# Update sums in the rows' own tiles, Fourier weights split ahead, and kept rows moved into the Fourier output projection

## The chip, the cores and the metric

The kernel runs on one core of a Trainium2 chip. The metric is the device time of one execution in microseconds (us); of several runs the median is given. The profile is one execution recorded by the hardware profiler. Engine names as the profile has them: PE is TensorE, PEld its weight loads, DVE is VectorE, ACT is ScalarE, POOL is GpSimd, SP is SyncE, which here only issues DMAs.

## The reference

Two layers on 512 latent tokens of 1024 channels (and 256 context tokens in layer 0). Each layer is: half-step SwiGLU FFN (width 2816), a token mixer, another half-step FFN. The mixer of layer 0 is windowed attention, that of layer 1 a Fourier mix. Each sub-layer's input is modulated, its output gated, added to the scaled input and normalised:

```
def post_norm_update(x, y, mod, j, g, b):
    gate = mod[:, 3 * j + 2][:, None, :]
    return layer_norm(ALPHA * x + gate * y, g, b)

def fourier_mix(h, w_o):                       # layer 1
    hg = h.reshape(B_, L_, FOURIER_GROUPS, FOURIER_GROUP_CH)     # 4 groups of 256 channels
    f = jnp.fft.fft2(hg, axes=(1, 3), norm="ortho").real
    return f.reshape(B_, L_, D_) @ w_o
...
        x = half_ffn_sublayer(x, mod_lat, 0, ffn_wi[i, 0], ffn_wo[i, 0], g[0], b[0])
        h = modulate(x, mod_lat, 1)
        y = ...                                # attention or fourier_mix
        x = post_norm_update(x, y, mod_lat, 1, g[1], b[1])
        x = half_ffn_sublayer(x, mod_lat, 2, ffn_wi[i, 1], ffn_wo[i, 1], g[2], b[2])
```

## The kernel before

All products are in float32 accuracy from three products of rounded halves: an operand is split into a high half (ScalarE copy, tiles `wh`, `uh`, `hh`, `ah`) and a low half (VectorE subtraction, `wl`, `ul`, `hl`, `al`), and `mm3` does high x high, low x high and high x low. Tokens are worked in four tiles of 128 rows. Helpers record every instruction, so the profile gives one line (L68) for nearly all; one goes by tile names.

**Slots.** Nearly all tiles in SBUF come from one pool of 42 equal slots (`SLOTS`, tag `slot`). A tile's slot comes free when its last reader is done; whoever needs one next waits for that. The pool also serves the raw weight loads, so loads are issued as slots come free.

**Weights.** `plan` lists all weight rows in the order of use: for the second layer the FFN's rows, then `w_t1` (one DFT table along channels), `w_t2` (four DFT tables along tokens), `w_fo` (eight rows of the Fourier output weights), then the last FFN. `weights(i, ahead)` (L176) makes sure that item i + ahead has been split, and loads raw rows (`wr`) two further. `gate_next` (L168) multiplies a raw row by a gate row (`wr<-wr,gr`) where a gate is folded into the weights, as it is for `w_fo`.

**Projection.** `project` (L459) computes y = u w: for the first rows f (the body) each row's product for all four token tiles, and the last `TAIL` = 4 rows token tile by token tile. Behind each token tile come `norm_stage` (L305: the sum `z` = ALPHA x + y and its statistics), `scale_stage` (z normalised in place) and `flip_stage` (products `tp` that turn it, the affine step `ht`, halves `hh` and `hl` for the next sub-layer). `z` is a slot of its own. In the body the look-ahead grows:

```
            self.weights(w0 + f, ahead=max(SPLIT_AHEAD, min(tail + 4, SPLIT_AHEAD + f - (body - 6))))
```

`project` returns two functions. `flip` turns the last token tile and is called during the next stage's first products. `keeps` loads two rows (`ln_g_row`, `ln_b_row`) and calls `keep_stage` (L372), which writes the new residual x = z g + b, two VectorE operations per token tile. In FFNs that follow, `keeps` is called at fixed pairs.

**Fourier stage** (L1135). Products `ab` with the channel table, evicted to `ah`, `al` and the Nyquist column `nyq`; then for each of four groups the cosine and sine products `f` along the tokens (group 0 also `pn` for the Nyquist rows), combined by four VectorE operations into `X`, with an edge row from `edge`. `stat` splits X of the group before into `uh` and `ul`. In this stage VectorE and ScalarE are pinned to the order of the code (`nc.pin(True)`); outside it a planner may move their instructions to where it expects a gap, within the dependencies. TensorE and GpSimd are pinned throughout. In that order stand, ahead of the groups, the split of the fourth token table and of `w_fo` rows 0 to 2 (`self.weights(w_fo + 2, ahead=0)`, L1177), and behind group 0 all four tiles of kept rows (`rest[1]()`, L1221). Then `project(w_fo, ...)` follows with a body of four rows.

Of the kernel before, what the change touches and what calls it, by code (L numbers as in the profile page):

```python
# [10 lines left out]
F32 = mybir.dt.float32  # L11
# [4 lines left out]
P = 128  # L16
D = 1024
KC = D // P
BLK = 32
BANK = 512  # L20
SEQ = 512
NT = SEQ // P
# [3 lines left out]
NF = DFF // P  # L26
# [13 lines left out]
SPLIT_AHEAD = 3  # L40
# [12 lines left out]
BETWEEN = 5  # L53
Q_TURN = 3
KEEP_AT = (5, 7, 9, 11)


class Pinned:
# [42 lines left out]
class Emitter:  # L101
# [203 lines left out]
    def norm_stage(self, st, t):  # L305
        nc = self.nc
        y, x = st["y"][t], st["x"][t]
        z = self.slot([P, 1024], F32, "z")
        stats = self.small([P, 2, 6], "bs")
        for h in range(2):  # L310
            sl = slice(h * 512, (h + 1) * 512)
            if "gate" in st:
                nc.vector.tensor_tensor(z[:, sl], y[:, sl], st["gate"][:, sl], ALU.mult)
                nc.vector.scalar_tensor_tensor(z[:, sl], x[:, sl], ALPHA, z[:, sl], ALU.mult, ALU.add)
            else:
                nc.vector.scalar_tensor_tensor(z[:, sl], x[:, sl], ALPHA, y[:, sl], ALU.mult, ALU.add)
            nc.vector.bn_stats(stats[:, h, :], z[:, sl])
        mv = self.small([P, 2], "mv")
        nc.vector.bn_aggr(mv, stats.rearrange("p a b -> p (a b)"))
        ve = self.small([P, 1], "ve")  # L320
        nc.vector.tensor_scalar(ve, mv[:, 1:2], EPS, None, ALU.add)
        rs = self.small([P, 1], "rs")
        nc.gpsimd.tensor_tensor(rs, ve, self.mhalf[:, 0:1], ALU.pow)
        st["n"][t] = (z, mv, rs)
# [131 lines left out]
                self.mod_steps(goal - self.n_job)  # L456


    def project(self, w0, nf, stat, st, ntok, mid=None, keep=True):  # L459
        mm = self.mm  # L460
        st["y"] = {}
        st["n"] = {}
        ss = {}

        def one(f, t, halfs=(0, 1)):
            w_hi, w_lo = self.parts[w0 + f]
            s_hi, s_lo = ss[f]
            if t not in st["y"]:
                st["y"][t] = self.bank2(nm="y")
            y = st["y"][t]  # L470
            sl = slice(t * P, (t + 1) * P)
            for i, (s, w) in enumerate(((s_hi, w_hi), (s_hi, w_lo), (s_lo, w_hi))):
                for half in halfs:
                    cs = slice(half * 512, (half + 1) * 512)
                    mm(y[:, cs], s[:, sl], w[:, cs], start=(f == 0 and i == 0), stop=(f == nf - 1 and i == 2))

        tail = TAIL if st["affine"] is not None else LAST_TAIL
        body = nf - tail
        for f in range(body):
            self.weights(w0 + f, ahead=max(SPLIT_AHEAD, min(tail + 4, SPLIT_AHEAD + f - (body - 6))))  # L480
            ss[f] = stat(f)
            if f == body // 2 and mid is not None:
                mid()
            for t in range(ntok):
                one(f, t)
            self.parts.pop(w0 + f)
        for f in range(body, nf):
            self.weights(w0 + f, ahead=nf + 3 - f)
            ss[f] = stat(f)
        self.nc.pin(st["affine"] is not None)  # L490
        for t in range(ntok):
            for half in range(2):
                for f in range(body, nf):
                    one(f, t, (half,))
            self.norm_stage(st, t)
            if st["affine"] is None:
                self.out_stage(st, t)
            elif t == 0:
                self.scale_stage(st, t)
            else:  # L500
                self.flip_stage(st, t - 1, lambda: self.scale_stage(st, t))
        self.nc.pin(False)
        for f in range(body, nf):
            self.parts.pop(w0 + f)

        def flip():
            v, a = self.nc.vector.on, self.nc.scalar.on
            self.nc.pin(True)
            self.flip_stage(st, ntok - 1)
            self.nc.vector.on, self.nc.scalar.on = v, a  # L510

        def keeps(i=None):

            if keep:
                if not i:
                    st["rows"] = self.ln_rows(*st["ln"])
                for t in range(ntok) if i is None else (i,):
                    self.keep_stage(st, t)

        return flip, keeps  # L520
# [21 lines left out]
        lo = self.hbuf([P, KC, SEQ], nm + "l")  # L542
        return [(hi, lo, 0, KC)]

    def half_step(self, ups, down, h, x, N, l, s, j, nxt, quota, first=None, halves=False, held=None, mid=None, out_h=None, keep=True, fold=True, more=None):

        us = []
        stat = self.halves_of(us, N)
        st = {}

        def late():
            self.mod_finish(self.n_job)
            gate = self.gate_row(l, s, j, 0.5)
            if fold:
                self.fold(gate, down, NF)
            else:
                st["gate"] = gate
            if more is not None:
                self.fold(self.gate_row(*more[0], 1.0), more[1], KC)
            stat(0)  # L560

        self.ffn_up(ups, h, N, quota, us, first=first, halves=halves, late=late, held=held)
        st["x"] = x() if callable(x) else x

        st["ln"] = (l, j)

        def middle():
            if mid is not None:
                mid()
            if keep and nxt is None:  # L570
                st["rows"] = self.ln_rows(l, j)

        st["affine"] = None if nxt is None else self.affine_ln(l, j, nxt[0], s, nxt[1])
        if nxt is not None:
            st["h"] = out_h() if out_h is not None else self.new_h("h")
        rest = self.project(down, NF, stat, st, N // P, mid=middle, keep=keep)
        return rest, st


# [135 lines left out]
    def run(self):  # L715
# [31 lines left out]
        w_l2 = ffn_items(2)  # L747
        w_t1 = add(ins["dft1"])
        w_t2 = add(*[ins["dft2"][i] for i in range(4)])
        w_fo = add(*[ins["fourier_wo"][k] for k in range(KC)])  # L750
# [9 lines left out]
        h, held = self.head()  # L760
# [7 lines left out]
        x = []  # L768
# [10 lines left out]
        def ctx_input():  # L779
# [17 lines left out]
        rest, st = self.half_step(  # L797
            w_l0[0], w_l0[1], h, load_x, SEQ, 0, 0, 0, (0, 1), 5 * KC, held=held, mid=ctx_input
        )
# [10 lines left out]
        def ctx_h():  # L810
# [11 lines left out]
        st = dict(x=x)  # L822
# [4 lines left out]
        rest = self.project(w_ao, KC, self.halves_of(oT, SEQ, KC), st, NT)  # L827
# [3 lines left out]
            w_l1[0], w_l1[1], st["h"], x, SEQ, 0, 0, 2, (1, 0), 5 * KC, first=rest, halves=True  # L831
        )
        rest, st = self.half_step(
            w_l2[0], w_l2[1], st["h"], x, SEQ, 1, 0, 0, (1, 1), 5 * KC, first=rest, halves=True, more=((1, 0, 1), w_fo)
        )

        fT = self.fourier(w_t1, w_t2, w_fo, st["h"], rest)
        st = dict(x=x)
        st["affine"] = self.affine_ln(1, 1, 1, 0, 2)
        st["h"] = self.new_h("h")  # L840

        st["ln"] = (1, 1)
        rest = self.project(w_fo, KC, fT, st, NT)


        rest, st = self.half_step(
# [288 lines left out]
    def fourier(self, w_t1, w_t2, w_fo, h, rest):  # L1135
# [38 lines left out]
        ny = (self.slot([P, NT, P], F32R, "nyh"), self.slot([P, NT, P], F32R, "nyl"))  # L1174
        self.split(ny[0], ny[1], nyq)
        t2 = [self.weights(w_t2 + i, ahead=3 - i) for i in range(4)]
        self.weights(w_fo + 2, ahead=0)  # L1177
        zero = self.slot([1, 256], F32, "zero")
        nc.gpsimd.memset(zero, 0.0)
        nh = SEQ // 2  # L1180
# [11 lines left out]
        for gr in range(FG):  # L1192
            ps, sine = (self.bank("f") for _ in range(2))
            for part, o in enumerate((ps, sine)):
                cs = slice(part * half, (part + 1) * half)

                def ops(t):
                    ah, al = ab[gr // 2, t // 2]
                    return ah[:, t % 2, gr % 2, cs], al[:, t % 2, gr % 2, cs]

                along(o[:, :n2], part, ops)
            if gr == 0:
                pn = self.bank("pn")
                along(pn[:, :n2], 0, lambda t: (ny[0][:, t], ny[1][:, t]))
            X = XX[:, gr]
            nc.scalar.copy(X[:, :, nh : nh + 1], ps[:, nh : nh + 1].unsqueeze(1).broadcast_to([P, 2, 1]))
            qs = self.slot([P, nh], F32, "qs")
            nc.scalar.copy(qs, sine[:, :nh])
            for i, (near, far) in enumerate(((ALU.subtract, ALU.add), (ALU.add, ALU.subtract))):
                nc.vector.tensor_tensor(X[:, i, :nh], ps[:, :nh], qs, near)  # L1210
                nc.vector.tensor_tensor(X[:, i, nh + 1 :], ps[:, nh - 1 : 0 : -1], qs[:, nh - 1 : 0 : -1], far)
            if gr == 0:
                edge = self.slot([P, n2], F32, "edge")
                nc.scalar.copy(edge, pn[:, :n2])
            row = edge[32 * gr : 32 * gr + 1]
            nc.scalar.copy(X[0:1, 1, : nh + 1], row[:, : nh + 1])
            nc.vector.tensor_tensor(X[0:1, 1, nh + 1 :], row[:, nh - 1 : 0 : -1], zero[:, : nh - 1], ALU.add)
            if gr > 0:
                stat(2 * gr - 2)
            if gr == 0:  # L1220
                rest[1]()  # L1221
        nc.pin(False)
        return stat

# [114 lines left out]
```

## Time and profile before

| | |
|---|---|
| median of 3 runs | 2053.14 us (2052.12 to 2055.15) |
| the profiled execution | 2051.99 us, its span 2050.0 us |
| granted TensorE clock, mean | 0.995 |
| TensorE busy | 2004.1 us (98%) |
| VectorE busy | 1324.0 us (65%) |
| ScalarE busy | 714.5 us (35%) |
| DMA | 292.56 MB, 143 GB/s mean |

A row of a timeline has the start in us from the start of the span, the length, the engine, the source line, the operation, output tile <- input tiles, shapes and count; in brackets the idle time of that engine before it and what ended it. In a row of a window table the stretch and its length stand first, then busy us (and instructions) of PE, PEld, DVE, ACT, POOL, then the granted clock of TensorE, the busy share of the DMA engines and GB/s. A row of the waits tells who waited for whom, the total, how often and the longest.

### The profile page before, as it was taken

What the parts mean: (1) busy time and instruction counts of PE and PEld (TensorE: products, weight loads), DVE (VectorE), ACT (ScalarE), POOL (GpSimd) and SP (SyncE); (2) the same over time, 40 slices, a digit from 0 to 9 for tenths busy, and PEclk for the clock granted to TensorE, in tenths of its full rate; (3) what the DMA queues carried; (4) which work ended last, traced back from release to release, by engine and by line L of the source; (5) the groups of instructions that cost most, each with busy time, mean ns of one, the idle gap of its engine ahead of it and who ended that gap; (6) DMA issues with size and microseconds to landing.
All of it is one profiled execution on the core that took longest, in us unless ns stands there. A gap on an engine that the chain in (4) does not pass through costs nothing.

```text
span 2050.0 us, 25222 instructions
## 1 busy us (share of the span) xinstructions
PE 2004.1 (98%) x9990; PEld 1684.2 (82%) x9990; DVE 1324.0 (65%) x1888; ACT 714.5 (35%) x1090; POOL 50.6 (2%) x56
## 2 busy tenths in 40 slices
PE   6999999999999999999999999999999699999998
PEld 5788888899888776888888888888888688888887
DVE  7659985698756887566558545765764873322754
ACT  3322233433634688322224322222432452222420
POOL 3000000000000300000000000000000000000000
PEclk9999999999999999999999999999999899999999
DMA  9656533387712012365543325654340323332321
GB/s 364 234 197 204 195 125 124 119 314 275 258 48 71 1 42 83 103 225 195 187 164 113 123 95 194 213 196 134 113 144 3 133 92 103 104 102 83 119 76 41
DMA packets 81910, 292.56 MB, mean 143 GB/s; under 512 B 9856, under 2 KB 10112, under 8 KB 81792
## 3 DMA queue, kind: packets, MB, share of 16 engines
q1 hardware_dynamic: 81792, 290.96, 41.4%
q8 instruction: 78, 1.28, 0.3%
q14 instruction: 40, 0.33, 0.0%
HBM read 288.83 MB, written 2.10 MB: 142 GB/s over the span
## 4 chain that ended last, share of the span: by engine, by line
PE 94%; DVE 4%; ACT 1%; issue 0%; DMA 0%; SPq 0%; DVEq 0%; ACTq 0%
PE up L68 52%; PE y L68 31%; PE qkv L68 4%; PE o L68 3%; PE s L68 1%; PE pt L68 1%; DVE acc L68 1%; PE tp L68 1%; DVE p L68 1%; DVE x L68 1%; PE ab L68 0%; PE qt L68 0%; DVE wr L68 0%; DMA wr<-in_wi_head_dram 0%; PE gp L68 0%
## 5 line engine op out<-in xcount | busy, mean ns | idle before, releaser
L68 DVE TENSOR_TENSOR wl<-wr,wh 128x1024 fp32r<-128x1024 f32 x356 | 426.0, 1219 | 108.4 <-ACT wh L68 74.0
L68 ACT CAST wh<-wr 128x1024 fp32r<-128x1024 f32 (+1 forms) x364 | 367.6, 1046 | 189.9 <-PE y L68 85.6
L68 PE MATMUL up<-hh,wh 128*128 128x512 f32 (+1 forms) x1152 | 429.4, 373 | 0.0
L68 PE MATMUL up<-hl,wh 128*128 128x512 f32 (+1 forms) x1152 | 427.9, 371 | 0.0
L68 PE MATMUL up<-hh,wl 128*128 128x512 f32 (+1 forms) x1152 | 427.8, 371 | 0.0
L68 PE MATMUL y<-wh,uh 128*128 128x512 f32 x920 | 303.8, 392 | 13.2 <-ACT X L68 13.2
L68 ACT ACTIVATE sg<-up 128x512 f32<-128x512 f32 (+1 forms) x110 | 61.1, 556 | 715.3 <-PE up L68 715.3
L68 PE MATMUL y<-wh,ul 128*128 128x512 f32 x920 | 302.6, 390 | 0.1
L68 PE MATMUL y<-wl,uh 128*128 128x512 f32 x920 | 302.3, 390 | 0.0
L68 DVE TENSOR_TENSOR u<-up,sg 128x512 f32<-128x512 f32 (+1 forms) x110 | 70.0, 637 | 354.1 <-PE up L68 353.8
L68 PEld LDWEIGHTS up<-hl,wh 128*128 128x128 f32 x1152 | 217.0, 188 | 37.5
L68 PEld LDWEIGHTS up<-hh,wl 128*128 128x128 f32 x1152 | 217.1, 188 | 37.2
L68 PEld LDWEIGHTS up<-hh,wh 128*128 128x128 f32 x1152 | 217.1, 188 | 36.9
L68 PEld LDWEIGHTS y<-wh,uh 128*128 128x128 f32 x920 | 173.4, 189 | 49.5 <-ACT uh L68 13.8
L68 PEld LDWEIGHTS y<-wh,ul 128*128 128x128 f32 x920 | 173.2, 188 | 36.6 <-DVE ul L68 0.6
L68 PEld LDWEIGHTS y<-wl,uh 128*128 128x128 f32 x920 | 173.3, 188 | 35.8
L68 DVE SCALAR_TENSOR_TENSOR acc<-mr,silu_c,acc 128x1024 f32<-128x1024 f32 x147 | 186.0, 1279 | 1.4
L68 PE MATMUL up<-h0h,wh 128*128 128x512 f32 x352 | 139.5, 396 | 3.0 <-ACT h0h L68 3.0
L68 DVE TENSOR_TENSOR wr<-wr,gr 128x1024 f32<-128x1024 f32 x104 | 124.5, 1219 | 22.3 <-DMA wr<-in_wo_dram 20.2
L68 PE MATMUL up<-h0l,wh 128*128 128x512 f32 x352 | 138.3, 393 | 0.0
L68 PE MATMUL up<-h0h,wl 128*128 128x512 f32 x352 | 138.1, 392 | 0.0
L68 DVE SCALAR_TENSOR_TENSOR z<-x,y 128x512 f32<-128x512 f32 x48 | 32.7, 682 | 125.1 <-PE y L68 125.0
(158 smaller groups left out, 2290.7 us busy)
## 6 DMA issues: line engine op xcount, KB each, us to landing
wr<-in_wi_dram SPq DMA_DIRECT2D x213, 512.0 KB, 4.4
mr<-in_mod_w_dram SPq DMA_DIRECT2D x144, 512.0 KB, 4.2
wr<-in_wo_dram SPq DMA_DIRECT2D x110, 512.0 KB, 3.6
m<-in_mod_head_dram SPq DMA_DIRECT2D x16, 512.0 KB, 8.0
wr<-in_wqkv_dram SPq DMA_DIRECT2D x12, 512.0 KB, 3.7
wr<-in_attn_wo_dram SPq DMA_DIRECT2D x8, 512.0 KB, 3.5
wr<-in_fourier_wo_dram SPq DMA_DIRECT2D x8, 512.0 KB, 5.4
wr<-in_wi_head_dram SPq DMA_DIRECT2D x8, 448.0 KB, 9.2
```

Of the source, the lines that this page charges most:

```text
L68: ins = f(*args, **kw)
```

## The change

Three edits. `norm_stage` writes the sum z into the tile of x where the gate is folded into the weights (everywhere but the context stream). `project` and `half_step` get a parameter `reach` in place of the constants of the look-ahead (`REACH` = 4 gives the old numbers), and the FFN ahead of the Fourier stage gets `REACH_DFT` = 9, by which its down projection splits the channel table, all four token tables and `w_fo` rows 0 to 3. The Fourier stage's own request for `w_fo` rows and its call of `keeps` go; `project(w_fo, ...)` gets `each=keeps`, which is called behind each of its four body rows f with f as the token tile.

```
+REACH = 4
+REACH_DFT = 9
...
     def norm_stage(self, st, t):
         nc = self.nc
         y, x = st["y"][t], st["x"][t]
-        z = self.slot([P, 1024], F32, "z")
+        z = self.slot([P, 1024], F32, "z") if "gate" in st else x
...
-    def project(self, w0, nf, stat, st, ntok, mid=None, keep=True):
+    def project(self, w0, nf, stat, st, ntok, mid=None, keep=True, reach=REACH, each=None):
...
         for f in range(body):
-            self.weights(w0 + f, ahead=max(SPLIT_AHEAD, min(tail + 4, SPLIT_AHEAD + f - (body - 6))))
+            self.weights(w0 + f, ahead=max(SPLIT_AHEAD, min(tail + reach, SPLIT_AHEAD + f - (body - 2 - reach))))
...
             self.parts.pop(w0 + f)
+            if each is not None:
+                each(f)
         for f in range(body, nf):
-            self.weights(w0 + f, ahead=nf + 3 - f)
+            self.weights(w0 + f, ahead=nf + reach - 1 - f)
...
         rest, st = self.half_step(
-            w_l2[0], w_l2[1], st["h"], x, SEQ, 1, 0, 0, (1, 1), 5 * KC, first=rest, halves=True, more=((1, 0, 1), w_fo)
+            w_l2[0], w_l2[1], st["h"], x, SEQ, 1, 0, 0, (1, 1), 5 * KC, first=rest, halves=True, more=((1, 0, 1), w_fo), reach=REACH_DFT
         )
+        keeps = rest[1]
         fT = self.fourier(w_t1, w_t2, w_fo, st["h"], rest)
...
-        rest = self.project(w_fo, KC, fT, st, NT)
+        rest = self.project(w_fo, KC, fT, st, NT, each=keeps)
...
     def fourier(self, w_t1, w_t2, w_fo, h, rest):
...
         t2 = [self.weights(w_t2 + i, ahead=3 - i) for i in range(4)]
-        self.weights(w_fo + 2, ahead=0)
...
-            if gr == 0:
-                rest[1]()
```

More of the change, by code (lines that the diff above doesn't have):

```diff
@@ L543, in new_h, with half_step @@
         return [(hi, lo, 0, KC)]
-    def half_step(self, ups, down, h, x, N, l, s, j, nxt, quota, first=None, halves=False, held=None, mid=None, out_h=None, keep=True, fold=True, more=None):
+    def half_step(self, ups, down, h, x, N, l, s, j, nxt, quota, first=None, halves=False, held=None, mid=None, out_h=None, keep=True, fold=True, more=None, reach=REACH):
         us = []
@@ L575, in half_step @@
             st["h"] = out_h() if out_h is not None else self.new_h("h")
-        rest = self.project(down, NF, stat, st, N // P, mid=middle, keep=keep)
+        rest = self.project(down, NF, stat, st, N // P, mid=middle, keep=keep, reach=reach)
         return rest, st
```

## The prediction

> **What bounds the kernel now.** I read the page's busy times first, then TensorE's waits, then the chain of waits around the longest one, then the engines' order in time there.
>
> ```profile
> PE 2004.1 (98%) x9990; PEld 1684.2 (82%) x9990; DVE 1324.0 (65%) x1888; ACT 714.5 (35%) x1090; POOL 50.6 (2%) x56
> ```
>
> TensorE is busy for 98% of the span, so an edit pays only where TensorE stands still or runs slowly. TensorE's waits in the stretch from the end of the second layer's first FFN to the last FFN, one row for each thing waited for (total, times, longest, us):
>
> ```profile
> PE y L68 <- ACT X L68: 13.2, 1, 13.2
> PE f L68 <- ACT qs L68: 1.1, 1, 1.1
> PE f L68 <- DVE wl L68: 0.8, 1, 0.8
> ```
>
> One wait is worth looking at: 13.2 us ahead of the first product y of the Fourier stage's output projection. The chain there, and the eight operations on x that stand in VectorE's queue at that place:
>
> ```profile
> 1630.34 1.04 ACT uh L68
> 1631.38 0.07 ACT X L68
> 1631.45 35.50 PE y L68 x144
> ```
> ```profile
> L68 DVE TENSOR_TENSOR x<-z,ln_g_row x4: 1206/1217/1218, 1619.2 to 1626.4; 128x1024 f32<-128x1024 f32 x4
> L68 DVE TENSOR_TENSOR x<-x,ln_b_row x4: 1224/1226/1226, 1620.4 to 1627.6; 128x1024 f32<-128x1024 f32 x4
> ```
>
> These are the kept rows (`keep_stage`): 1619.2 to 1628.8, 9.6 us, between the sums X of Fourier group 0 and those of group 1. The projection needs uh, the high half of X, and that stands behind group 1's X. In time order TensorE shows the following (start, length, operation):
>
> ```profile
> L68 PE MATMUL f<-wh,ah x32: 277/283/388, 1602.5 to 1617.7; 128*128 128x258 f32 x32
> ```
> ```profile
> 1606.55 0.28 PE L68 MATMUL pn<-wh,nyh 128*128 128x258 f32 x1
> ...
> 1607.87 0.28 PE L68 MATMUL pn<-wl,nyh 128*128 128x258 f32 x1
> ```
> ```profile
> 1617.96 0.28 PE L68 MATMUL f<-wl,ah 128*128 128x258 f32 x1
> 1631.43 1.22 PE L68 MATMUL y<-wh,uh 128*128 128x512 f32 x2 [13.20 <-ACT X L68]
> ...
> 1636.72 0.73 PE L68 MATMUL y<-wh,uh 128*128 128x512 f32 x2
> ...
> 1638.22 0.62 PE L68 MATMUL y<-wh,uh 128*128 128x512 f32 x2
> ...
> 1645.02 0.61 PE L68 MATMUL y<-wh,uh 128*128 128x512 f32 x2
> ```
>
> Before the wait: twelve pn products start over 1.32 us, 0.12 us each. Behind it: the first six pairs of y take 5.29 us (1631.43 to 1636.72), while fifteen later pairs take 6.80 us (1638.22 to 1645.02), 0.453 us each. The granted clock says why (PEclk is the third figure from the end):
>
> ```profile
> 1622.00:1624.00 2.00, 0.00 (x0) 0.00 (x0) 1.97 (x3) 0.00 (x0) 0.00 (x0) 0.82 0.95 387
> 1624.00:1626.00 2.00, 0.00 (x0) 0.00 (x0) 1.97 (x3) 0.00 (x0) 0.00 (x0) 0.50 0.17 70
> 1636.00:1638.00 2.00, 2.00 (x9) 1.60 (x8) 1.97 (x6) 0.45 (x2) 0.00 (x0) 0.76 0.00 0
> ```
>
> TensorE idles from 1618.2, the clock is halved at about 1623 and comes back at about 1637.
>
> **Part 1, kept rows out of the Fourier stage.** They leave the place between X of group 0 and X of group 1 and go into the projection, one token tile behind each of the first four weight rows. **Part 2, the weights split ahead.** Up to five more items (the last DFT table and rows 0 to 3 of the output weights) get their high and low halves during the down projection before. These two parts have one answer together. Without them the products f and pn (96 + 12) run through: 1602.5 + 108 x 0.12 = 1615.5. What they then wait for must be there. Sine products of group 0 end at 1602.5 + 24 x 0.12 = 1605.4, those of group 1 at 1602.5 + 60 x 0.12 = 1609.7. VectorE's cadence for one group, once the kept rows are done, is seen here:
>
> ```profile
> 1628.76 1.40 DVE L68 TENSOR_TENSOR X<-f,qs 128x256 f32<-128x256 f32 x4
> 1630.19 0.41 DVE L68 TENSOR_TENSOR X<-edge,zero 1x255 f32<-1x255 f32 x1
> 1631.41 1.23 DVE L68 TENSOR_TENSOR ul<-X,uh 128x1024 fp32r<-128x1024 f32 x1 [0.81 <-ACT uh L68]
> 1632.56 1.41 DVE L68 TENSOR_TENSOR X<-f,qs 128x256 f32<-128x256 f32 x4
> ```
>
> That is 3.8 us a group. So X of group 1 starts at about 1610.2 (half a microsecond for qs), group 2 at 1614.0, group 3 at 1617.8 to 1619.2. uh of group 0 follows group 1's X as in the chain above (uh ends 2.6 us behind the start of X there), at about 1613: ahead of 1615.5. The last token tile of the first y row needs the PSUM banks of group 3, at 1615.6 + 18 x 0.227 = 1619.7, half a microsecond after they come free. So y starts at about 1615.6 and not at 1631.4: 15.8 us, of which 13.2 is the idle gap and the rest the two f waits and the gaps at their edges. The half clock goes too, because nothing idles for microseconds: 5.29 us plus 0.57 for the next pair against 7 x 0.453 = 3.17 is 2.7 us. Sum of what can be had: 18.5 us.
>
> [...]
>
> **What it costs elsewhere: VectorE's debt.** The kept rows now stand between the projection's first products and its norms, so I add VectorE up by stage (busy us of TensorE, its weight loads, VectorE, ScalarE):
>
> ```profile
> 1603.00:1618.20 15.20, 13.33 (x106) 12.71 (x104) 12.41 (x14) 5.40 (x9) 0.01 (x1) 1.00 0.29 104
> 1618.20:1631.40 13.20, 0.04 (x1) 0.00 (x0) 12.10 (x16) 2.19 (x7) 0.00 (x0) 0.69 0.64 231
> 1631.40:1659.00 27.60, 27.57 (x110) 22.65 (x111) 22.17 (x27) 13.37 (x18) 0.00 (x0) 0.90 0.30 100
> ```
> ```profile
> 1609.30 3.49 DVE L68 TENSOR_TENSOR wr<-wr,gr 128x1024 f32<-128x1024 f32 x3
> ...
> 1647.06 6.90 DVE L68 TENSOR_TENSOR wl<-wr,wh 128x1024 fp32r<-128x1024 f32 x6
> ...
> 1661.54 0.69 DVE L68 SCALAR_TENSOR_TENSOR z<-x,y 128x512 f32<-128x512 f32 x1 [1.30 <-PE y L68]
> ```
> ```profile
> 1664.37 1.25 ACT L68 ACTIVATE z<-z,nm,rs 128x1024 f32<-128x1024 f32 x1 [11.46 <-DVE nm L68]
> ```
>
> From 1603 to the first norm VectorE does 12.4 + 12.1 + 22.2 = 46.7 us. Part 2 takes out one split and four gate-and-split pairs, nine operations at 1.15 (6.90/6): 10.4. Left are 36.3 us. Room: the first turning products tp stood 35.5 us behind the start of y (the 144 products in the chain's last row); less the 2.7 of half clock that is 1615.6 + 32.8 = 1648.4. z must be scaled by then. The second half of the first norm starts at 1661.54 and z is scaled at 1665.6, 4.1 us; a VectorE that comes late has the first half's sum and statistics to do as well, 1.4 us at 0.69 each, so it must be free by 1648.4 - 5.5 = 1642.9. That is 39.9 us for 36.3. It fits only if VectorE idles less than 3.6 us, and the group chain forces idle time: per group 0.8 for uh (the row of ul above) and some 0.4 for the edge row, about 4.4 in all, beside the wait for group 1. The gaps ahead of group 1 can be filled with gates and splits of later rows: in the row at 1609.30 two of the three gates belong to rows that the program asks for only in the projection, so the planner does pull such work forward. Bounds: nothing, if three or four of those 1.15 us operations fill gaps; if none does, pinned work ends at 1617.8 + 3.9 = 1621.7, and 9.6 kept rows, 4 gates, 8 splits and the last ul (13 x 1.15 = 15.0) end at 1646.3, 3.4 us late. I take 1.0, near the lower end, since the trace shows such filling.
>
> **Part 2's own cost.** Five items more in the down projection: nine VectorE operations (10.4 us), five ScalarE casts. Their cover:
>
> ```profile
> 1567.68 0.69 DVE L68 SCALAR_TENSOR_TENSOR z<-x,y 128x512 f32<-128x512 f32 x1 [22.50 <-PE y L68]
> ```
> ```profile
> 1533.18 56.56 SPq L164 DMA_DIRECT2D wr<-in_fourier_wo_dram  x5
> ```
>
> VectorE idles 22.5 us ahead of that projection's first norm, and five raw rows were issued from 1533 on (the last by 1589.7): cost nothing. If the cover is gone (no slot for the halves), the splits stay in the Fourier stage; that is a rival. Slots at the end of that projection, counted from the code: x 4, gate row 1, uh and ul 4, its own weights 8, split DFT and output weights 18, raw rows 2: 37 of 42. On the SP queue the two row loads (ln_g, ln_b) move behind output rows 6 and 7 and ahead of the last FFN's; the t1 halves free slots from 1602.5, so they land by about 1615 and are wanted at 1621. POOL's queue keeps its order. The longer reach only moves the start of the ramp from the 14th to the 8th row; the other calls keep the old numbers.
>
> **Part 3, sums into x.** z takes x's tile: the same operations on the same shapes, no time; four slots less per update. The norm now waits on the kept row's tile, which it read before too.
>
> Sum: -18.5 + 1.0 = -17.5. The profiled execution, 2051.99, becomes 2034.5; the median of the three runs stands 1.15 higher, 2053.14, and gives 2035.6. Less than 0.2% (4 us) is no change that a measurement can tell.
>
> **Rivals.** (A) VectorE's debt is paid in full: nothing fills the gaps, the first tp waits 3.4 us, and from there on VectorE is nearly full in each token step, so it does not catch up. For: the 3.6 us of slack above. Against: the pulled-forward gates. [...] (B) The halves do not get ahead: with slots full (that fifth raw row waited till the y products ended) splits stay where they were, and only the kept rows leave the chain: 9.6, and the clock's 2.7 since 3.6 us of idle remain. 2053.1 - 12.3 = 2040.8; without the clock 2043.5. (C) Slower: the down projection becomes bound by weight preparation. Its ramp starts six rows earlier, two items a row, and each extra pair of halves takes slots from raw rows; VectorE already waits for loads there:
>
> ```profile
> 1506.29 1.23 DVE L68 TENSOR_TENSOR wr<-wr,gr 128x1024 f32<-128x1024 f32 x1 [2.54 <-DMA wr<-in_wo_dram]
> ```
>
> If each of eleven rows comes late by more than 18.5/11 = 1.7 us the kernel is slower; at the 2.54 of this row, 2053.1 - 17.5 + 28 = 2064. Against: VectorE's 22.5 us of idle afterwards shows the rows are prepared well ahead, and TensorE never waits there.
>
> **Chances.** Forecast (2034 to 2037.5) 0.63; A 0.14; B 0.13; C 0.07; no effect 0.03. The range 2033.5 to 2042.5 holds the forecast, A and most of B, about 0.85 less their edges; its low end is the 18.5 in full from the fastest run shown. Faster 0.90, same 0.03, slower 0.07.
>
> **What would show it.** Right: no wait of y for X; y starts within half a microsecond of the last f, some 13 us behind the first; clock 1.00 throughout; kept rows between weight splits; first tp 32.8 to 34 us behind y's start. Wrong: a tp wait over 3 us (A), wl of output rows 0 to 3 still among the f products (B), TensorE waiting for wl or wh in the down projection (C), or a second halving of the clock.

## The result

The changed kernel takes 2039.2 us (median of 4 runs, 2039.18 to 2041.12) against 2052.97 us of the kernel before (4 runs in the same comparison): a ratio of 0.9934, 95% interval 0.9921 to 0.9946, so 13.8 us faster. The profiled execution took 2039.18 us, its span is 2037.3 us.

The page's busy times of the changed kernel, to be held against the same row of before: the same work on every engine in a span that is 12.7 us shorter.

```profile
PE 2003.1 (98%) x9990; PEld 1683.6 (83%) x9990; DVE 1324.4 (65%) x1888; ACT 714.4 (35%) x1090; POOL 50.5 (2%) x56
```

TensorE's waits around the Fourier stage (who waited for whom, total, how often, longest, us). Before there were four, the three shown in the prediction and the 0.7 us of ab. Now there are two; the wait for X and the waits of f are gone, and a new one stands in their place, 3.4 us for `ul`:

```profile
PE y L70 <- DVE ul L70: 3.4, 1, 3.4
PE ab L70 <- DVE al L70: 0.7, 1, 0.7
```

The chain of waits through the stage (start, length, what). Products ab, f, pn and y follow one another without a gap; y breaks once, for the last `ul`, which stands behind weight splits and kept rows. The chain leaves y already at 1637.6, to follow what ended last on VectorE, so 10 of the 144 products are in none of its rows; the row below the chain, from TensorE's own timeline, shows the break. It comes after 104 products, 23.6 us behind y's start:

```profile
1600.02 3.14 PE ab L70 x24
1603.16 2.90 PE f L70 x24
1606.06 1.45 PE pn L70 x12
1607.51 8.70 PE f L70 x72
1616.21 21.38 PE y L70 x94
...
1638.56 2.35 DVE wl L70 x2
1640.91 1.14 DVE x L70
1642.05 1.14 DVE ul L70
1643.19 0.04 issue
1643.23 11.01 PE y L70 x40
1654.24 0.87 PE tp L70 x8
```
```profile
1643.23 0.50 PE L70 MATMUL y<-wh,ul 128*128 128x512 f32 x1 [3.40 <-DVE ul L70]
```

For all comparisons below I use one stage: from the start of the last 24 products ab to the first tp of the projection. In the chain of before it lasted 1666.95 - 1599.57 = 67.4 us:

```profile
1599.57 3.15 PE ab L68 x24
...
1666.95 0.87 PE tp L68 x8
```

After the change it lasts 1654.24 - 1600.02 = 54.2 us. So 13.2 us of the gain lie here; the changed kernel's execution reaches the stage 0.45 us later, and behind it the two differ by nothing that counts. Had y run through, the stage would have lasted 16.2 us to y's start and 32.7 for 144 products at 0.227: 48.9 us. The new wait costs 5.3 of that: 3.4 us of idle TensorE, and 40 products in 11.01 us instead of 9.1, at a granted clock of 0.68 and then 0.50 (PEclk is the third figure from the end):

```profile
1641.00:1643.00 2.00, 0.00 (x0) 0.00 (x0) 2.00 (x2) 0.00 (x0) 0.00 (x0) 1.00 0.37 150
1643.00:1645.00 2.00, 1.76 (x5) 1.43 (x6) 1.35 (x3) 0.00 (x0) 0.00 (x0) 0.68 0.00 0
1645.00:1647.00 2.00, 2.00 (x6) 1.54 (x6) 1.35 (x2) 0.00 (x0) 0.00 (x0) 0.50 0.00 0
```

VectorE's order there (start, length, operation, count). The last `ul` stands behind three kept rows and a half, eight splits and two gates that follow the `ul` of 1621.14 without any idle time:

```profile
1621.14 1.23 DVE L70 TENSOR_TENSOR ul<-X,uh 128x1024 fp32r<-128x1024 f32 x1 [0.81 <-ACT uh L70]
1622.29 2.36 DVE L70 TENSOR_TENSOR wl<-wr,wh 128x1024 fp32r<-128x1024 f32 x2
1624.56 2.35 DVE L70 TENSOR_TENSOR wr<-wr,gr 128x1024 f32<-128x1024 f32 x2
1626.83 1.22 DVE L70 TENSOR_TENSOR x<-x,ln_g_row 128x1024 f32<-128x1024 f32 x1
...
1640.83 1.22 DVE L70 TENSOR_TENSOR x<-x,ln_g_row 128x1024 f32<-128x1024 f32 x1
1641.96 1.22 DVE L70 TENSOR_TENSOR ul<-X,uh 128x1024 fp32r<-128x1024 f32 x1
1643.10 1.22 DVE L70 TENSOR_TENSOR x<-x,ln_b_row 128x1024 f32<-128x1024 f32 x1
```

### The profile page after: what moved, and what is told of

The parts are those of the page before. It is cut to its first block, busy times and chain, and to the rows that moved or that the text cites. A ratio compares the mean times of both kernels' runs of the same rounds, so it can differ in the third digit from the quotient of the medians.

```text
span 2037.3 us, 25228 instructions
## 1 busy us (share of the span) xinstructions
PE 2003.1 (98%) x9990; PEld 1683.6 (83%) x9990; DVE 1324.4 (65%) x1888; ACT 714.4 (35%) x1090; POOL 50.5 (2%) x56
## 4 chain that ended last, share of the span: by engine, by line
PE 94%; DVE 4%; issue 0%; ACT 0%; DMA 0%; SPq 0%; DVEq 0%
PE up L70 52%; PE y L70 31%; PE qkv L70 4%; PE o L70 2%; DVE p L70 1%; DVE acc L70 1%; PE s L70 1%; PE pt L70 1%; PE tp L70 1%; PE f L70 1%; PE ab L70 0%; PE qt L70 0%; DVE wl L70 0%; DMA wr<-in_wi_head_dram 0%; PE gp L70 0%
## 5 line engine op out<-in xcount | busy, mean ns | idle before, releaser
L70 DVE SCALAR_TENSOR_TENSOR x<-x,y 128x512 f32<-128x512 f32 x48 | 32.7, 682 | 105.3 <-PE y L70 105.3
```

The costliest lines, as they stand in the source:

```text
L70: ins = f(*args, **kw)
```

## The experiments

Two theories of the new wait: (1) order: the last `ul` is wanted by row 6 of the projection and stands too far back in VectorE's queue; (2) amount: VectorE has too much to do in the projection, and whatever stands last is late. Each run was compared with the kernel before on the same chip. Times of one kernel scatter by 0.7 to 4.9 us in one comparison, in the profiled executions mostly from a lower clock in the attention stage (0.91 over 20 us in five of thirteen; last section), so the stage's duration is given beside the median.

| kernel | median us | stage us | waits of y or tp in it, us |
|---|---|---|---|
| before | 2052.97 | 67.4 | X 13.2 |
| changed | 2039.2, again 2039.03 | 54.2, again 54.2 | ul 3.4 |
| last ul at the end of the Fourier stage | 2035.09, again 2035.59 | 49.7, again 49.7 | tp 0.9 |
| look-ahead two rows shorter | 2036.05 | 50.3 | ul 1.1 |
| both | 2037.64, again 2034.4 | 48.9, again 48.9 | none |
| rows 4 and 5 in the idle stretch, last ul early | 2035.35 | 50.2 | X 1.0 |
| look-ahead two rows longer | 2043.06 | 56.3 | ul 5.7 |
| kept rows back (part 2 without 1) | 2041.48 | 55.7 | X 4.4 and 0.2 |
| weights back (part 1 without 2) | 2050.55 | 65.5 | X 3.7, ul 6.0 |
| z in its own slot | 2039.68 | 54.2 | ul 3.4 |

**The last ul first.**

```
         # end of fourier()
+        stat(2 * FG - 2)
         nc.pin(False)
```

> Edit on the changed kernel: the last pair of X (rows 6 and 7 of the projection) is split into uh and ul at the end of the Fourier stage, pinned, instead of behind the kept rows and the splits of the next FFN. Theory 1 (order in VectorE's queue): the wait of y for ul (3.4 us at 1639.8) goes and the clock is not halved behind it; VectorE still ends its work ahead of the norms at about 1644.3, some 0.9 us later than the first tp allows, so the first tp stands about 33.7 us behind y's start and the kernel takes about 2034.7. Theory 2 (VectorE simply has too much to do, wherever it stands): the same 3.4 us and the halved clock come back ahead of the first tp, 2038 to 2040.

Measured: 2035.09 us (2034.74 to 2035.45), ratio to before 0.9912 (0.9895 to 0.9929). TensorE's wait for `ul` is gone, and one of 0.9 us stands at the first tp:

```profile
PE tp L70 <- ACT x L70: 0.9, 1, 0.9
```

Theory 1 holds for the 3.4 us and the clock: an edit that changes only the order of work gives back 4.5 of the 5.3 us. (It moves ScalarE's cast of the high half `uh` too, but in the changed kernel that was done by 1632.8, long before y wanted it.) Theory 2 holds for the rest: VectorE reaches the norms 0.9 us late though `ul` stands first.

**Look-ahead two rows shorter.**

```
-        rest = self.project(w_fo, KC, fT, st, NT, each=keeps)
+        rest = self.project(w_fo, KC, fT, st, NT, each=keeps, reach=2)
```

> Edit on the changed kernel: the Fourier output projection looks ahead by two rows less (reach 2 there alone), so that two splits of the last FFN's weights (2.3 us of VectorE) come behind the norms. Theory 1 and 2 agree that ul then ends 2.3 us earlier: y waits about 1.1 us instead of 3.4. Whether the clock is halved tells them apart from a third reading: if the clock falls only after idling longer than about 3 us, it stays at 1.00 and the time is about 2034.9; if any wait of a microsecond brings it down, about 2037.

Measured: 2036.05 us (2034.83 to 2037.8), the wait as expected, and the clock stays whole behind it:

```profile
PE y L70 <- DVE ul L70: 1.1, 1, 1.1
```
```profile
1644.00:1646.00 2.00, 2.00 (x11) 1.64 (x10) 1.28 (x2) 0.00 (x0) 0.00 (x0) 1.00 0.00 0
```

So behind 1.1 us of idle TensorE the granted clock here was 1.00, behind the changed kernel's 3.4 us it fell to 0.50. The median is 1.1 us above what was expected for the unhalved clock, though the stage is 3.9 us shorter than the changed kernel's; its profiled run entered the stage 1.7 us later than the changed kernel's, so in that run the excess lies ahead of the edit (one event of the kind in the last section).

**Look-ahead two rows longer** (`reach=6` in the same place).

> The suspected cost enlarged on the changed kernel: the projection looks ahead by two rows more (reach 6), two more splits of the next FFN's weights stand ahead of the last ul. Theory 1: the last ul ends 2.3 us later, y waits 5.7 us instead of 3.4 with the clock halved as before or a little longer: 2041 to 2042.5. If the wait is set by something else than VectorE's queue (a transfer, a bank), it stays at 3.4 us and 2039.

Measured: 2043.06 us (2042.66 to 2045.19), half a microsecond above the range given; its stage, 56.3 us, is 2.1 us longer than the changed kernel's, as 2.3 us of splits ask. The profiled run entered the stage 4.0 us later than the changed kernel's, with two such events.

```profile
PE y L70 <- DVE ul L70: 5.7, 1, 5.7
```

Two rows less, as many more: the wait is 1.1, 3.4 and 5.7 us, a step of 2.3 us each, which is two VectorE operations of 1.15. In all three traces VectorE works without a pause from the `ul` before to the last one, so its queue sets the wait.

**Part 2 without part 1: kept rows back.**

```
+            if gr == 0:
+                rest[1]()                       # in fourier(), as before
-        rest = self.project(w_fo, KC, fT, st, NT, each=keeps)
+        rest = self.project(w_fo, KC, fT, st, NT)
```

> Part 2 without part 1: weights split ahead and sums in x as in the changed kernel, but all kept rows back behind group 0 of the Fourier stage. If the kept rows set y's start: they run from about 1609 to 1618.5, X of group 1 and uh follow, y starts at about 1621.5 to 1622 after some 6 us of idle TensorE with the clock halved, no wait for ul later: 2042 to 2045. If the split weights carried the gain, it stays near 2039.

Measured: 2041.48 us (2040.99 to 2042.28), slightly below the range; the wait is 4.4 us and not 6, because y starts at 1621.3, in an execution that entered the stage 0.7 us later than the changed kernel's. The chain shows the kept rows in their old place, and no wait for `ul` follows:

```profile
1609.08 1.22 DVE x L70
...
1617.50 1.23 DVE x L70
...
1627.72 28.68 PE y L70 x125
1656.40 0.87 PE tp L70 x8
```

**Part 1 without part 2: weights back.**

```
-REACH_DFT = 9
+REACH_DFT = 4
...
+        self.weights(w_fo + 2, ahead=0)         # in fourier(), as before
```

> Part 1 without part 2: kept rows in the projection and sums in x as in the changed kernel, the last token table and the output weights split inside the Fourier stage as before. Theory 1 and 2 (VectorE's debt): y starts about 9.6 us earlier than before (1621.9), but VectorE then has about 33.5 us to do until the last ul, which y needs 23.6 us behind its start: y waits some 10 us there and the clock is halved, so that nothing is left of the gain, 2051 to 2055. If parts simply add (9.6 us and the clock's 2.7 gone): 2041.

Measured: 2050.55 us (10 runs, 2050.06 to 2054.7), ratio 0.9989 (0.998 to 0.9998), half a microsecond below the range given. Both waits are there:

```profile
PE y L70 <- DVE ul L70: 6.0, 1, 6.0
PE y L70 <- ACT X L70: 3.7, 1, 3.7
```

Moving the kept rows alone is worth 1.9 us of the stage, not 12: y starts 9.6 us earlier than before and then stands for the queue that took their place. The wait is 6.0 us and not the 10 expected: the chain gives 1654.0 for the end of the last `ul`, 32 us behind y's start, and the halved clock at y's start (0.50 from 1624 to 1626 in this trace) had made y slower too, which I had not counted as cover.

So the changed kernel's 13.2 us divide into 11.7 for the weights split ahead (67.4 to 55.7) and 1.5 for the kept rows behind that (55.7 to 54.2); in the other order they are 1.9 for the kept rows and 11.3 for the weights. Once `ul` stands first, the kept rows' part is 6.0 (55.7 to 49.7).

**Part 3 undone: z in its own slot.**

> Part 3 undone alone: z gets a slot of its own again in every update, the rest as in the changed kernel. If the sums in x are worth only slots, and the slots only matter where halves do not fit: with 4 slots less the raw rows of the projection and of the next FFN come later, and either nothing waits for them (2039 to 2040) or y waits for wl of rows 6 and 7 or ul later than before (2041 to 2046). If the sum written in place made the operations themselves cheaper or dearer, the norm rows would show it.

```
-        z = self.slot([P, 1024], F32, "z") if "gate" in st else x
+        z = self.slot([P, 1024], F32, "z")
```

Measured: 2039.68 us (2038.72 to 2042.03); the stage and the wait are the changed kernel's. The sums in x neither cost nor give time in this kernel, and at a look-ahead of 9 the four slots that they free were not what the halves needed. The operation takes the same 0.68 us in place (the changed kernel's tile x, median 684 ns) as it did before (`z<-x,y`, 683 ns):

```profile
L70 DVE SCALAR_TENSOR_TENSOR x<-x,y x8: 670/684/691, 1645.0 to 1667.2; 128x512 f32<-128x512 f32 x8
```

**Splits in the idle stretch.** In the changed kernel VectorE stands idle for 2.4 us behind group 0 of the Fourier stage:

```profile
1608.05 0.41 DVE L70 TENSOR_TENSOR X<-edge,zero 1x255 f32<-1x255 f32 x1
1610.85 1.41 DVE L70 TENSOR_TENSOR X<-f,qs 128x256 f32<-128x256 f32 x4 [2.39 <-ACT qs L70]
```

```
+        for j in (w_fo + 4, w_fo + 5):          # ahead of the stage: their gates
+            self.load_raw(j + 1)
+            nc.vector.tensor_tensor(self.raws[j], self.raws[j], self.row_of.pop(j), ALU.mult)
...
+            if gr == 0:
+                self.weights(w_fo + 5, ahead=0)
...
+        stat(2 * FG - 2)
```

> On the changed kernel: last pair of X split at the end of the Fourier stage, and the splits of output rows 4 and 5 pinned into VectorE's idle stretch behind group 0 of the Fourier stage (2.4 us idle in the changed kernel's trace), their gates ahead of the stage. If that stretch stood empty because the planner had no free slots for the halves, the two splits wait for slots here too, X of group 1 comes later and y with it: above 2036. If slots are free there, 2.3 us of VectorE's work are gained, the first tp no longer waits 0.9 us: about 2034.2.

Measured: 2035.35 us (2034.77 to 2038.85), stage 50.2 against 49.7 without this edit. Neither reading holds whole. The splits found slots (they run in the stretch, waiting only 0.88 us for ScalarE's cast), so a lack of slots is not shown to be why it stood empty; but they push X of group 1 back by 0.8 us, and with the rows split earlier the planner also put two gates between the groups, each of which pushes X back by another 0.4 (4.2 us a group instead of 3.8):

```profile
1613.06 2.36 DVE L70 TENSOR_TENSOR wl<-wr,wh 128x1024 fp32r<-128x1024 f32 x2 [0.88 <-ACT wh L70]
1615.33 1.41 DVE L70 TENSOR_TENSOR X<-f,qs 128x256 f32<-128x256 f32 x4
1616.66 1.22 DVE L70 TENSOR_TENSOR wr<-wr,gr 128x1024 f32<-128x1024 f32 x1
```

The tp wait went, and y waits 1.0 us for X instead. Why the planner leaves the stretch empty in the changed kernel stays open.

**Both edits: last ul first, look-ahead two rows shorter.**

> Both edits on the changed kernel: last pair of X split at the end of the Fourier stage, and the projection's look-ahead two rows shorter. Theory 1 (what is left after the first edit is the 0.9 us wait of the first tp, because VectorE comes 0.9 us late to the norms): with 2.3 us of splits taken from ahead of the norms that wait goes, y runs 32.8 us to the first tp without a break, about 2034.2. Rival: the two splits now fall between norms and flips, where VectorE is busy 6.1 of 6.3 us in each token step, and a later tp or the first products of the next FFN wait for them: 2035 to 2037.

The first time this took 2037.64 us (2033.39 to 2038.25) though its trace had no wait in the stage: 48.9 us, as worked out above for y without a break. It was run again, beside the changed kernel and the first edit:

> That edit and the look-ahead shorter by two rows once more: its first trace had the stage at 48.9 us without a wait, but the time, 2037.64, was not the lowest. If the excess was a lower granted clock in the attention stage, which the edit does not touch, the runs without it lie near 2033.5 and the median below that of the edit before by about 0.9 us. If the edit itself costs something later, all its runs lie at 2037 or more.

> The edit with the last pair of X split at the end of the Fourier stage once more: stage 49.8 us, the first tp waiting 0.9 us; 4.4 us below the changed kernel's median of the same call, 2035 to 2037.

> The changed kernel once more, beside the two edits below on the same chip. Runs so far scatter by 2 to 4 us, which the traces put ahead of the Fourier stage. Expected 2039 to 2041, the stage from the last ab products to the first tp 54.2 us as in its first trace.

Measured: 2034.4 us (2032.73 to 2034.61), ratio to before 0.9904 (0.9891 to 0.9918); the first edit alone 2035.59 us (2034.69 to 2038.71); the changed kernel 2039.03 us (2038.17 to 2041.2). The chain of the second run, in which y runs through to the first tp:

```profile
1606.45 8.70 PE f L70 x72
1615.15 32.70 PE y L70 x144
1647.85 0.87 PE tp L70 x8
```

This run is 18.4 us below before and 4.6 below the changed kernel. By the stage it is the version to keep, 0.8 us shorter than the first edit alone in both pairs of traces; the medians do not settle it (2037.64 against 2035.09 the first time, 2034.4 against 2035.59 the second). The two splits that now fall behind the norms make nothing wait: its trace has no TensorE wait from 1590 to 1700 but the 0.7 us of ab.

## Why the prediction was right, and where its size was off

The direction and the cause held; the forecast was 2035.6 and the kernel takes 2039.2. That lies outside the 2034 to 2037.5 given a chance of 0.63, and inside the range of 2033.5 to 2042.5, which was made wide enough to take in rival A. By its steps:

- **The kept rows and the splits set y's start; 18.5 us can be had.** Right. y was put at 1615.6 and starts at 1616.2, in an execution that reached the stage 0.45 us later. The 18.5 us were all there: with the last `ul` first and the look-ahead two rows shorter the stage shrinks from 67.4 to 48.9, which is 18.5. That y's start needs both parts was right as well: with either alone y still waits for X, 4.4 and 3.7 us. In time they are worth 11.7 and 1.9 us alone, and 13.2 together, no more than the sum, as long as the last `ul` stands where it does.
- **The group's cadence of 3.8 us and the PSUM banks.** Right: X starts at 1610.85, 1614.66, 1618.48 in the changed kernel, and y does not wait for the banks of group 3.
- **VectorE's debt, taken at 1.0 us.** This is the term that was mis-sized: it measured 5.3 us. What failed is the deadline. The whole debt was held against one, the first tp. The last `ul` was counted in the sum (the last of 13 operations) without its own deadline, which comes first: y wants it after 104 products, 23.6 us behind its start, while the norms leave VectorE 27 us. Against the first tp alone 1.0 us was about right: with `ul` first, that product waited 0.9 us. But this came out by another way than argued. The planner put none of the hoped-for operations into the gaps between the groups; it put two gates of this work into the down projection, so VectorE ended at 1644.3, against 1646.3 for the bound with nothing pulled. And the 0.4 us of idle time per group for the edge row was misread: that row is VectorE's own work, and VectorE idles 0.8 us a group. In all it idled 7.2 us of the 41.3 from 1603 to 1644.3, nearly all of it ahead of the `ul` of 1621.14:

```profile
1603.00:1616.05 13.05, 13.05 (x111) 13.05 (x110) 7.66 (x18) 4.81 (x14) 0.00 (x0) 1.00 0.29 106
1616.05:1644.30 28.25, 24.85 (x110) 20.16 (x109) 26.45 (x28) 11.78 (x15) 0.00 (x0) 0.99 0.52 194
```

- **The clock.** The sum took the halved clock as gone, and the prediction named a second halving as a sign of being wrong. It came, and gave back 1.9 us, not the 2.7 of before. The sum has no term for it. In the changed kernel's trace the granted clock was 0.50 behind 3.4 us of idle, with the look-ahead two rows shorter 1.00 behind 1.1; in the attention stage it also fell, to 0.70, behind a wait of 1.85 us (last section), so in these traces the length alone does not decide.
- **Cover in the down projection.** Right: VectorE's idle time ahead of that projection's norm fell from 22.5 to 5.0 us, and TensorE never waited there for `wl` or `wh`.

```profile
1568.14 0.69 DVE L70 SCALAR_TENSOR_TENSOR x<-x,y 128x512 f32<-128x512 f32 x1 [4.97 <-PE y L70]
```

- **Rivals.** A came nearest in time: with its 3.4 us in place of the 1.0 the sum is 2053.1 - 18.5 + 3.4 = 2038.0, and 2040.7 if the 2.7 us of the halved clock are not had; these stand on either side of the 2039.2. Nothing filled the gaps, as it says, but the wait that it names, 3.4 us at the first tp, was not there; that the wait for `ul` has the same length is chance. B did not happen: no output row's split is left among the f products. That 3.6 us of idle would have left B the clock whole is not what the runs show: with the weights back y waited 3.7 us for X, and the granted clock was 0.50 from 1624 to 1626. C did not happen. (By the code the ramp starts with the 9th row and not the 8th, five rows earlier than before and not six.)

## What to carry to other kernels

Work that is moved off one wait lands in a queue; give every operation in that queue its own deadline, in the order in which the consumer wants them, and not the queue's total one deadline at its end. An operation that a lazy helper issues where it is first asked for (here the last `ul`) comes late when other work is put in front of it: issue it where its input is ready. Count an idle stretch as cover only if the trace shows what will fill it.

## What the runs showed of the hardware that was not expected

TensorE's granted clock fell behind a wait in one run and stayed whole behind the same wait in another. In the attention stage, which neither of these two edits touches, TensorE waits about 1.85 us in all kernels (it is busy 18.13 to 18.15 of the 20 us from 680 to 700 in all thirteen profiled executions). In the first run of both edits, 1.85 us at the products s, the granted clock was 0.73 and 0.70 over 3 us each; in the run with the last `ul` first, 1.87 us at the same products, it was 1.00. The same microseconds of the two, the first two rows of both edits, the third of the last `ul` first:

```profile
688.00:691.00 3.00, 1.66 (x7) 1.66 (x8) 2.95 (x7) 1.68 (x4) 1.58 (x2) 0.73 0.00 0
691.00:694.00 3.00, 3.00 (x10) 1.97 (x10) 2.78 (x11) 2.89 (x10) 2.92 (x4) 0.70 0.00 0
```
```profile
688.00:691.00 3.00, 2.15 (x14) 1.84 (x15) 3.00 (x8) 1.66 (x5) 2.07 (x3) 1.00 0.00 0
```

Two such events stand in that run (0.91 of full clock over 680 to 700 and again over 780 to 800, there behind a wait of 1.4 us; each is worth 20 x 0.09 = 1.8 us), and it entered the Fourier stage 3.5 us later than the run without. Five of the thirteen profiled executions show one or two such events; what decides whether one comes is not shown. Their cost is as large as several of the edits measured here, so a stage's own duration tells more than one execution's time.
